# Layer norms as two fused VectorE operations, and the second expert result added by an accumulating DMA

## The chip, the cores and the metric

One core of one Trainium2 chip runs the whole program. The metric is device microseconds of one execution, as the median of several. The core has five engines that work side by side, each through its own instructions in order: TensorE (PE, whose weight loads are listed as PEld), VectorE (DVE), ScalarE (ACT), GpSimd (POOL) and SyncE (SP), which here only starts transfers. SP, ACT and POOL can all start DMAs; those of POOL have a queue of their own.

## What is computed

Two layers on 2048 tokens of 1024 numbers. Each layer has a mixer and then a mixture of experts, and after each of the two a residual and a layer norm. The first mixer is attention, the second a pooling over the last 2, 4, 8 or 16 tokens. Cut to what matters here:

```python
def layer_norm(x, g, b):
    mu = jnp.mean(x, axis=-1, keepdims=True)
    var = jnp.mean(jnp.square(x - mu), axis=-1, keepdims=True)
    return (x - mu) * lax.rsqrt(var + LN_EPS) * g + b

for i in range(2):
    f = mla_mixer(x, ...) if i == 0 else pool_mixer(x, ...)
    x = layer_norm(ALPHA * x + f, ln_g[i, 0], ln_b[i, 0])
    f = hier_moe(x, ...)          # two experts of 64 for each token, their results weighted and added
    x = layer_norm(ALPHA * x + f, ln_g[i, 1], ln_b[i, 1])
```

## The kernel before

The work runs in stages, one after the other: projections, attention, `output_projection`, the experts of layer 0, `pool_layer`, the experts of layer 1, `last_norm`. `output_projection` and `pool_layer` go over 16 tiles of 128 tokens. A tile's work is a Python generator; `run_slots` starts one tile every three slots and advances all of them one step per slot, so that the steps of some nine tiles are interleaved. A scheduler behind the program then puts each engine's instructions into one order, and buffers (`bufs=` of a tile) decide how far loads may run ahead.

The experts write their two weighted results for a token to two halves of a table `Y` in HBM. `pool_layer` does the following for a tile.

- `residual` (L1093) loads the two results (`rya`, `ryb`) and the residual (`rx`) with three DMAs on SP. POOL adds `ryb` to `rya` (L1103). DVE makes `rya = ALPHA*rx + rya` and the row sums (L1106).
- `normalize` (L968): DVE turns the sum into minus the mean (`lnnm`), ACT squares `rya - mean` and sums (L978), DVE makes the inverse deviation `lnrs` (L980 and `rsqrt`, L197: three Newton steps on 128x1 columns), then `lnnb = lnnm*lnrs` (L983), and ACT writes the normalized tile (L985).
- POOL multiplies the normalized tile by `ag` into `pres` (L1194). PE pools it with band matrices (`rpt`, L1201 and L1204), ACT copies that (`pooled`, L1206), PE multiplies it by the pool weights (`pz`, L1212 and L1216), and DVE adds it to `pres` in two halves (L1218).
- The second norm `n2` (class `Norm`, L988) is `normalize` on `pres` with a multiplication by `lng` on POOL (L1003; on DVE for the last tile alone) and an addition of `lnb` on DVE (L1005). The result is stored from ACT's queue.
- PE transposes the result (L1015), and the router (L496) chooses experts: a matmul (`plog`, L501), and some twenty small DVE instructions (`lg` to `ov`, L504 to L570) with two exponentials on ACT, a running count `ohsum` on POOL (L552) and a table on PE (`ptab`, L572).

`output_projection` uses the same `Norm` and the same router, and `last_norm` has the fused norm already, with `rsqrt`. While the last tiles of `pool_layer` run, SP loads the weights of three experts of layer 1.

Of the kernel before, what the change touches and what calls it, by code (L numbers as in the profile page):

```python
# [63 lines left out]
LN_EPS = 1e-5  # L64
# [132 lines left out]
def rsqrt(nc, pool, v):  # L197

    e, n = nc.vector, v.shape[1]
    y = pool.tile([P, n], I32, name="rsq_y", bufs=4)  # L200
    e.tensor_scalar(y, v.bitcast(I32), -0.5, 1597463007.0, op0=ALU.mult, op1=ALU.add)
    yf = y.bitcast(F32)
    h = pool.tile([P, n], F32, name="rsq_h", bufs=4)
    e.tensor_scalar(h, v, -0.5, None, op0=ALU.mult)
    t = pool.tile([P, n], F32, name="rsq_t", bufs=4)
    for i in range(3):
        if n == 1:
            e.tensor_scalar(t, yf, yf, h, op0=ALU.mult, op1=ALU.mult)
# [756 lines left out]
        self.ctx.close()  # L965


def normalize(nc, w, z, total):  # L968

    nm = w.tile([P, 1], F32, name="lnnm", bufs=4)  # L970
    if total.shape[1] == 2:
        nc.vector.tensor_scalar(nm, total[:, 0:1], total[:, 1:2], -1.0 / D, op0=ALU.add, op1=ALU.mult)
    else:
        nc.vector.tensor_scalar(nm, total, -1.0 / D, None, op0=ALU.mult)
    yield
    sq = w.tile([P, D], BF16, name="lnsq", bufs=1)
    rs = w.tile([P, 1], F32, name="lnrs", bufs=4)
    nc.scalar.activation(sq, z, AF.Square, bias=nm, accum_out=rs)  # L978
    yield
    nc.vector.tensor_scalar(rs, rs, 1.0 / D, LN_EPS, op0=ALU.mult, op1=ALU.add)  # L980
    rsqrt(nc, w, rs)
    nb = w.tile([P, 1], F32, name="lnnb", bufs=4)
    nc.vector.tensor_tensor(nb, nm, rs, op=ALU.mult)  # L983
    yield
    nc.scalar.activation(z, z, AF.Identity, bias=nb, scale=rs)  # L985


class Norm:  # L988
# [7 lines left out]
        queue.dma_start(self.g, g.partition_broadcast(P))  # L996
        queue.dma_start(self.b, b.partition_broadcast(P))

    def __call__(self, dst, z, total, engine=None):
        nc = self.nc  # L1000
        yield from normalize(nc, self.work, z, total)
        yield
        (engine or nc.gpsimd).tensor_tensor(z, z, self.g, op=ALU.mult)  # L1003
        yield
        nc.vector.tensor_tensor(dst, z, self.b, op=ALU.add)  # L1005


def transposed(nc, c, ps, work, x, out):
# [32 lines left out]
def output_projection(tc, c, I, wo, OT, X1, rt_pool, prefetch):  # L1041

    nc = tc.nc
    with ExitStack() as ctx:
# [13 lines left out]
        def token_tile(t):  # L1058
            sl = slice(t * P, (t + 1) * P)
            o = os[t % 2]  # L1060
            if t:
                wo.load(o, OT, t)
            z = w.tile([P, D], F32, name="z", bufs=4)
            loads.append(nc.sync.dma_start(z, I["x"][sl, :]))
            total = w.tile([P, 2], F32, name="total", bufs=4)
            yield
            for half in range(2):
                pz = ps.tile([P, 512], F32, name="pz", bufs=3)
                hs = slice(half * 512, half * 512 + 512)
                n = 0  # L1070
                for k in range(ND):
                    for a, b in ((0, 0), (1, 0), (0, 1)):
                        nc.tensor.matmul(pz, o[:, a, k, :], wo.parts[k][b][:, hs], start=(n == 0), stop=(n == 3 * ND - 1))  # L1073
                        n += 1
                yield
                nc.vector.scalar_tensor_tensor(z[:, hs], z[:, hs], ALPHA, pz, op0=ALU.mult, op1=ALU.add,
                                               accum_out=total[:, half:half + 1])
            yield from norm(z, z, total, nc.vector if t == NT - 1 else None)
            nc.scalar.dma_start(X1[sl, :], z)
            yield  # L1080
            xT = []
# [11 lines left out]
def residual(nc, w, X, Y, sl, out, loads):  # L1093
# [1 line left out]
    t0 = sl.start  # L1095
    ya = w.tile([P, D], F32, name="rya", bufs=6)
    nc.sync.dma_start(ya, Y[sl, :])
    yb = w.tile([P, D], F32, name="ryb")
    loads.append(nc.sync.dma_start(yb, Y[t0 + S:t0 + S + P, :]))
    x = w.tile([P, D], F32, name="rx")  # L1100
    nc.sync.dma_start(x, X[sl, :])
    yield
    nc.gpsimd.tensor_tensor(ya, ya, yb, op=ALU.add)  # L1103
    yield
    total = w.tile([P, 1], F32, name="rtotal", bufs=4)
    nc.vector.scalar_tensor_tensor(ya, x, ALPHA, ya, op0=ALU.mult, op1=ALU.add, accum_out=total)  # L1106
# [66 lines left out]
def pool_layer(tc, c, I, mixer, X1, Y, X3, rt_pool, prefetch):  # L1173

    nc = tc.nc
    with ExitStack() as ctx:
# [8 lines left out]
        def token_tile(t):  # L1185
# [5 lines left out]
            yield from normalize(nc, w, x2, total)  # L1191
            yield
            r = w.tile([P, D], F32, name="pres", bufs=4)
            nc.gpsimd.tensor_tensor(r, x2, ag, op=ALU.mult)  # L1194
            pp = w.tile([P, ND, P], F32, name="pooled")
            for half in range(2):
                pt = ps1.tile([P, 4, P], F32, name="rpt", bufs=2)
# [11 lines left out]
            for half in range(2):  # L1209
# [7 lines left out]
                yield  # L1217
                nc.vector.scalar_tensor_tensor(r[:, hs], pz.rearrange("p a b -> p (a b)"), 1.0, r[:, hs],  # L1218
                                               op0=ALU.mult, op1=ALU.add, accum_out=total[:, half:half + 1])
            yield from n2(r, r, total, nc.vector if t == NT - 1 else None)  # L1220
            nc.scalar.dma_start(X3[sl, :], r)
            yield
            xT = []
# [310 lines left out]
def last_norm(tc, c, Y, xs, norm, out):  # L1534

    nc = tc.nc
    with tc.tile_pool(name="fin", bufs=3, reuse_waits="tile") as w, tc.tile_pool(name="fin_ps", bufs=4, space=PSUM, reuse_waits="tile") as ps:

        def pair(n):
# [26 lines left out]
                nc.scalar.activation(sq, z[:, i], AF.Square, bias=nm[:, i:i + 1], accum_out=rs[:, i:i + 1])  # L1566
                nc.vector.scalar_tensor_tensor(o[:, i], z[:, i], nm[:, i:i + 1], norm.g, op0=ALU.add, op1=ALU.mult)
            yield
            nc.vector.tensor_scalar(rs, rs, 1.0 / D, LN_EPS, op0=ALU.mult, op1=ALU.add)
            rsqrt(nc, w, rs)  # L1570
            for i in range(2):
                nc.vector.scalar_tensor_tensor(o[:, i], o[:, i], rs[:, i:i + 1], norm.b, op0=ALU.mult, op1=ALU.add)
                nc.scalar.dma_start(out[t0 + i * P:t0 + (i + 1) * P, :], o[:, i])
# [114 lines left out]
```

## Time and profile before

| | us |
|---|---|
| median of 3 runs (3017.34 to 3025.28) | 3017.5 |
| the profiled execution: its own time | 3011.0 |
| the profiled execution: from the first to the last instruction (the span) | 3009.2 |
| busy in the span: PE / DVE / POOL / ACT | 2675.4 / 1482.6 / 1029.1 / 861.0 |
| `output_projection`, from about 1200 to | 1448 |
| experts of layer 0, to about | 2052 |
| `pool_layer`, to about | 2320 |
| experts of layer 1, to about | 2893 |

Times in the profile are counted from the first instruction of one profiled execution. "Busy" is time in which an engine had an instruction in work; an instruction that is held up after it started counts as busy. The granted clock is TensorE's clock as a share of 2.4 GHz. A row of the timeline has the start, the duration, the engine, the line of the kernel and what is written and read; in square brackets stands how long the engine was idle before it and what ended that.

### The profile page before, as it was taken

The page shows a single profiled execution, that of the slowest core. Times are in us where ns is not written, and L with a number is a line of the kernel's source. Part 1 is how long each engine was busy: PE and PEld are TensorE (multiplying, and loading weights), DVE is VectorE, ACT ScalarE, POOL GpSimd, SP SyncE. Part 2 cuts the span into 40 slices and gives each one's busy share as a digit, 9 for nine tenths or more (in the row PEclk, how much of TensorE's full clock was granted, in tenths as well). Part 3 has the DMA queues.
Part 4 walks back from the last instruction along what each step waited for, and adds up shares of the span by engine and source line. Part 5 has one row for each costly group of instructions (what it writes and reads, how often), then busy time and mean ns, then how long its engine had stood idle before and what let it go on. Part 6 is the DMA issues. An engine that isn't in the chain of part 4 may idle for free.

```text
span 3009.2 us, 50823 instructions
## 1 busy us (share of the span) xinstructions
PE 2675.4 (89%) x19378; PEld 1499.0 (50%) x19378; DVE 1482.6 (49%) x3717; ACT 861.0 (29%) x1465; POOL 1029.1 (34%) x877
## 2 busy tenths in 40 slices
PE   6987988889889899999799998996887999999976
PEld 6874545545555455888333333334776333333323
DVE  7645767667778675446321111315997121111118
ACT  4444434344444434223111111113452111111102
POOL 4244656566666546211111111114542111111100
PEclk9998999999999999999799999997897999999989
DMA  6544122121221212646699999985415999999967
GB/s 206 192 153 161 58 71 68 61 75 59 78 71 58 68 33 88 189 144 231 253 419 417 411 410 358 419 353 217 161 64 232 359 419 417 414 409 411 417 263 289
DMA packets 230242, 690.22 MB, mean 229 GB/s; under 512 B 42318, under 2 KB 102990, under 8 KB 180588
## 3 DMA queue, kind: packets, MB, share of 16 engines
q1 hardware_dynamic: 191484, 586.01, 51.2%
q0 software_dynamic: 27104, 69.90, 6.1%
q10 hardware_dynamic: 11408, 31.02, 2.7%
q8 instruction: 155, 2.54, 0.3%
q14 instruction: 91, 0.75, 0.1%
HBM read 595.47 MB, written 120.71 MB: 238 GB/s over the span
## 4 chain that ended last, share of the span: by engine, by line
PE 55%; DMA 23%; DVE 13%; issue 4%; ACT 3%; POOL 2%; SPq 1%; ACTq 0%; DVEq 0%; POOLq 0%; another core or an unknown queue 0%
DMA w<-in_w_dram 15%; PE ph L1336 13%; PE sc L678 9%; PE py L1364 6%; PE po L678 6%; PE pz L1073 5%; PE pm L678 5%; DVE mx L800 3%; PE pt L1324 2%; PE pt L368 2%; PE pl L325 2%; PE plog L501 2%; DMA R<-rl 1%; DMA qn<-QN 1%; DMA rl<-R 1%
## 5 line engine op out<-in xcount | busy, mean ns | idle before, releaser
L1336 PE MATMUL ph<-w,xT 128*32 128x512 f32 x5888 | 680.5, 602 | 41.1 <-DMA w<-in_w_dram 41.0
L1336 PEld LDWEIGHTS ph<-w,xT 128*32 128x32 f32 x5888 | 198.9, 111 | 450.0 <-issue 427.3
L1293 POOL DMA_INDIRECT Y<-y,idst x92 | 91.9, 998 | 936.6 <-ACT xT L1325 874.5
L800 DVE TENSOR_REDUCE mx<-pm 128x2 f32<-128x1024 f32 (+2 forms) x320 | 339.5, 1061 | 116.1 <-PE pm L678 110.9
L903 POOL TENSOR_TENSOR acc<-acc,pe 128x512 f32<-128x512 f32 (+3 forms) x256 | 311.0, 1215 | 207.5 <-ACT pe L889 194.4
L889 ACT ACTIVATE pe<-sc 128x1024 f32<-128x1024 f32 (+1 forms) x320 | 280.0, 896 | 355.7 <-DVE sc L887 202.2
L1341 DVE SCALAR_TENSOR_TENSOR h<-sg,gate,ph 128x256 f32<-128x256 f32 x92 | 44.2, 480 | 658.8 <-ACT sg L1339 658.8
L1364 PE MATMUL py<-w,hT 128*32 128x512 f32 x2944 | 347.9, 592 | 1.6 <-DVE hT L1351 1.6
L678 PE MATMUL sc<-qn,k 64*128 64x512 f32 (+2 forms) x1920 | 260.1, 376 | 20.8 <-ACT rl L846 15.5
L678 PE MATMUL po<-pe,vt 128*64 128x512 f32 (+3 forms) x1280 | 277.8, 557 | 0.0
L1339 ACT ACTIVATE sg<-ph 128x256 f32<-128x256 f32 x92 | 35.4, 384 | 727.0 <-PE ph L1336 715.0
L902 DVE TENSOR_TENSOR acc<-acc,pe 128x512 f32<-128x512 f32 (+3 forms) x256 | 226.3, 884 | 11.0 <-ACT pe L889 10.0
L1364 PEld LDWEIGHTS py<-w,hT 128*32 128x32 f32 x2944 | 106.1, 110 | 214.3 <-issue 210.1
L678 PEld LDWEIGHTS sc<-qn,k 64*128 64x128 f32 x1920 | 176.8, 195 | 66.7 <-ACT rl L846 20.6
L678 PE MATMUL pm<-k,qn 64*128 64x512 f32 (+2 forms) x640 | 146.4, 451 | 70.0 <-DVE mx L800 64.4
L1366 DVE COPY y<-py 128x512 f32<-128x512 f32 x92 | 63.6, 692 | 224.4 <-PE py L1364 224.4
L678 PEld LDWEIGHTS pm<-k,qn 64*128 64x128 f32 x640 | 64.7, 194 | 188.6 <-DVE mx L800 98.8
L678 PEld LDWEIGHTS po<-pe,vt 128*64 128x64 f32 x1280 | 80.3, 140 | 131.8 <-issue 123.5
L1324 PEld LDWEIGHTS pt<-ident,xg 128*128 128x128 f32 x736 | 90.4, 194 | 97.4 <-issue 72.9
L1324 PE MATMUL pt<-ident,xg 128*128 128x128 f32 x736 | 108.2, 291 | 23.2 <-DMA xg<-X,isrc 21.9
L678 PE MATMUL pm<-ka,qa 64*128 64x512 f32 (+2 forms) x640 | 124.9, 382 | 0.0
L678 PE MATMUL sc<-qb,kb 33*128 33x512 f32 (+2 forms) x640 | 121.4, 371 | 0.0
(364 smaller groups left out, 4331.3 us busy)
## 6 DMA issues: line engine op xcount, KB each, us to landing
w<-in_w_dram SPq DMA_DIRECT2D x384, 1024.0 KB
fy<-Y SPq DMA_DIRECT2D x16, 1024.0 KB
OT<-ot SPq DMA_DIRECT2D x31, 512.0 KB
K<-kq SPq DMA_DIRECT2D x32, 256.0 KB
V<-v SPq DMA_DIRECT2D x16, 512.0 KB
QN<-kq SPq DMA_DIRECT2D x32, 256.0 KB
qn<-QN SPq DMA_DIRECT2D x32, 256.0 KB
qb<-QR SPq DMA_DIRECT2D x128, 64.0 KB
```

The costliest lines, as they stand in the source:

```text
L325: nc.tensor.matmul(pl, a[:, k, :], w[:, k, :], start=(k == 0 and n == 0), stop=(k == ND - 1 and n == 2))
L678: return self.pin(self.nc.tensor.matmul(*a, **kw))
L800: self.pin(nc.vector.tensor_reduce(mx[:, :, tt, ch], pm[:, :, :n], axis=AX.X, op=ALU.max))
L889: nc.scalar.activation(pe[:, :, c0:], sc[:, :, c0:], AF.Exp, scale=SCALE)
L902: self.pin(self.nc.vector.tensor_tensor(acc[:, 0, c0:], before[:, 0, c0:], pe[:, 0, c0:], op=ALU.add))
L903: self.nc.gpsimd.tensor_tensor(acc[:, 1, c0:], before[:, 1, c0:], pe[:, 1, c0:], op=ALU.add)
L1073: nc.tensor.matmul(pz, o[:, a, k, :], wo.parts[k][b][:, hs], start=(n == 0), stop=(n == 3 * ND - 1))
L1293: st = self.nc.gpsimd.indirect_dma_start(out=self.Y, out_offset=bass.IndirectOffsetOnAxis(ap=idx, axis=0), in_=y, in_offset=None, bounds_c ...
L1324: self.pin(nc.tensor.transpose(pt[:, j, :], x[:, half * 4 + j, :], self.c.ident))
L1336: self.pin(nc.tensor.matmul(ph[js], xT[:, k, js], w[:, :, k, :], start=(k == 0), stop=(k == ND - 1), tile_position=(0, j * n)))
L1364: self.pin(nc.tensor.matmul(py[js], hT[:, k, js], w[:, k, hs], start=(k == 0), stop=(k == NF - 1), tile_position=(0, j * n)))
L1366: (nc.vector.tensor_copy if half else nc.scalar.copy)(y[:, hs], py)
```

## The change

The norms of class `Norm` (the one in `output_projection` and the second one in `pool_layer`) lose the ACT pass that normalizes: `(z - mean)*g` and `(..)*rs + b` are each one DVE instruction. Everywhere the inverse deviation starts from a scaled column and needs one DVE instruction less. In `pool_layer` the multiplication by `ag` goes from POOL to DVE, and the addition of the second expert result is no instruction of an engine any more: a DMA started by POOL adds it to `rya` in place, once the first result has landed there.

```diff
+def inverse_deviation(nc, pool, v):
+    e, n = nc.vector, v.shape[1]
+    h = pool.tile([P, n], F32, name="rsq_h", bufs=4)
+    e.tensor_scalar(h, v, -0.5 / D, -0.5 * LN_EPS, op0=ALU.mult, op1=ALU.add)
+    y = pool.tile([P, n], I32, name="rsq_y", bufs=4)
+    e.tensor_scalar(y, h.bitcast(I32), -0.5, 519526879.0, op0=ALU.mult, op1=ALU.add)
...
-def normalize(nc, w, z, total):
+def minus_mean(nc, w, total):
     nm = w.tile([P, 1], F32, name="lnnm", bufs=4)
...
+def squares(nc, w, z, nm):
...
     nc.scalar.activation(sq, z, AF.Square, bias=nm, accum_out=rs)
+    return rs
+
+def normalize(nc, w, z, total):
+    nm = minus_mean(nc, w, total)
     yield
-    nc.vector.tensor_scalar(rs, rs, 1.0 / D, LN_EPS, op0=ALU.mult, op1=ALU.add)
-    rsqrt(nc, w, rs)
+    rs = squares(nc, w, z, nm)
+    yield
+    inverse_deviation(nc, w, rs)
...
-    def __call__(self, dst, z, total, engine=None):
+    def __call__(self, dst, z, total):
         nc = self.nc
-        yield from normalize(nc, self.work, z, total)
+        nm = minus_mean(nc, self.work, total)
         yield
-        (engine or nc.gpsimd).tensor_tensor(z, z, self.g, op=ALU.mult)
+        rs = squares(nc, self.work, z, nm)
         yield
-        nc.vector.tensor_tensor(dst, z, self.b, op=ALU.add)
+        inverse_deviation(nc, self.work, rs)
+        nc.vector.scalar_tensor_tensor(z, z, nm, self.g, op0=ALU.add, op1=ALU.mult)
+        nc.vector.scalar_tensor_tensor(dst, z, rs, self.b, op0=ALU.mult, op1=ALU.add)
...
     nc.sync.dma_start(ya, Y[sl, :])
-    yb = w.tile([P, D], F32, name="ryb")
-    loads.append(nc.sync.dma_start(yb, Y[t0 + S:t0 + S + P, :]))
+    nc.gpsimd.dma_start(ya, Y[t0 + S:t0 + S + P, :], accum_op=ALU.add)
     x = w.tile([P, D], F32, name="rx")
-    nc.sync.dma_start(x, X[sl, :])
+    loads.append(nc.sync.dma_start(x, X[sl, :]))
     yield
-    nc.gpsimd.tensor_tensor(ya, ya, yb, op=ALU.add)
     yield
...
             r = w.tile([P, D], F32, name="pres", bufs=4)
-            nc.gpsimd.tensor_tensor(r, x2, ag, op=ALU.mult)
+            nc.vector.tensor_tensor(r, x2, ag, op=ALU.mult)
...
             yield
-            nc.vector.tensor_scalar(rs, rs, 1.0 / D, LN_EPS, op0=ALU.mult, op1=ALU.add)
-            rsqrt(nc, w, rs)
+            inverse_deviation(nc, w, rs)
```

The scheduler orders the changed program anew. On POOL, in the middle of `pool_layer`, this was one tile's work before, from one running count `ohsum` to the next:

```order
L552 TENSOR_TENSOR ohsum_19083<-ohsum_19083,ohb 128x64
L1003 TENSOR_TENSOR pres<-pres,lng_19073 128x1024
L1103 TENSOR_TENSOR rya<-rya,ryb 128x1024
L1194 TENSOR_TENSOR pres<-rya,ag 128x1024
L552 TENSOR_TENSOR ohsum_19083<-ohsum_19083,ohb 128x64
```

And this is POOL in the changed program, from the start of the stage on (the lines are those of the changed file; L1128 is the accumulating DMA, L571 the running count):

```order
628 L1128 DMA rya<-Y_62 128x1024 x9
629 L571 TENSOR_TENSOR ohsum_19016<-ohsum_19016,ohb 128x64
630 L1128 DMA rya<-Y_62 128x1024 x2
631 L571 TENSOR_TENSOR ohsum_19016<-ohsum_19016,ohb 128x64
632 L1128 DMA rya<-Y_62 128x1024
```

The three wide instructions per tile are gone, and the running counts stand behind DMA starts, the first one behind nine of them.

On DVE, in the middle of the stage, this is a piece of one tile's work before: router instructions (`es` to `oh`, and `ohp`, `ov`), with the addition of `lnb` and the two additions to `pres` and `rya` between them.

```order
2466 L523 TENSOR_REDUCE es<-esel 128x8
2467 L568 TENSOR_SCALAR ohp<-iota,rpos_19086 128x192
2468 L525 MAX em<-es 128x8
2469 L570 TENSOR_TENSOR ov<-oh,rval_19087 128x128
2470 L527 MAX_INDEX ei<-em,es 128x8
2471 L1005 TENSOR_TENSOR pres<-pres,lnb_19074 128x1024
2472 L529 SCALAR_TENSOR_TENSOR rexp_19085<-gf,ei 128x2
2473 L1218 SCALAR_TENSOR_TENSOR pres,ptotal<-pz,pres 128x512
2474 L533 TENSOR_SCALAR nem<-em 128x1
2475 L546 TENSOR_SCALAR oh<-iota,rexp_19085 128x64 x2
2476 L980 TENSOR_SCALAR lnrs<-lnrs 128x1
2477 L1106 SCALAR_TENSOR_TENSOR rya,rtotal<-rx,rya 128x1024
```

And a piece of one tile's work in the changed program, with the multiplication by `ag` (L1222) and the first of the two fused operations of the norm (L1034; the second, L1035, stands 20 rows on):

```order
2413 L1222 TENSOR_TENSOR pres<-rya,ag 128x1024
2414 L525 MAX gm<-lg 128x8
2415 L583 SCALAR_TENSOR_TENSOR rk,rpos_19019<-oh,plog 128x64
2416 L527 MAX_INDEX gi<-gm,lg 128x8
2417 L533 TENSOR_SCALAR ngm<-gm 128x1
2418 L583 SCALAR_TENSOR_TENSOR rk,rpos_19019<-oh,plog 128x64
2419 L529 CAST gf<-gi 128x1
2420 L219 TENSOR_SCALAR rsq_h<-lnrs 128x1
2421 L1034 SCALAR_TENSOR_TENSOR pres<-pres,lnnm,lng_19006 128x1024
2422 L531 TENSOR_SCALAR goh<-iota,gf 128x8
2423 L222 TENSOR_SCALAR rsq_y<-rsq_h 128x1
2424 L1246 SCALAR_TENSOR_TENSOR pres,ptotal<-pz,pres 128x512
```

Two 1024-wide instructions per tile stood here; now there are four (L1134, which is L1106 of before, L1222, L1034 and L1035), and the instructions of `lnrs` stand between them and the router's.

## Rows read from the trace of the kernel before

**Rows 1.** Windows view: busy us (instructions) of PE, PEld, DVE, ACT, POOL; clock, DMA share, GB/s.

```profile
1276.00:1348.00 72.00, 72.00 (x398) 62.27 (x397) 36.02 (x227) 21.52 (x46) 13.78 (x11) 1.00 0.49 149
2052.00:2144.60 92.60, 68.20 (x393) 60.11 (x393) 73.47 (x213) 40.45 (x63) 54.77 (x23) 0.80 0.64 233
2144.60:2221.20 76.60, 61.10 (x383) 53.93 (x381) 76.56 (x292) 37.02 (x73) 37.70 (x20) 0.91 0.35 122
2221.20:2320.00 98.80, 82.30 (x500) 74.31 (x498) 87.11 (x434) 42.87 (x90) 29.61 (x23) 0.84 0.42 167
2320.00:2893.00 573.00, 544.00 (x4807) 201.67 (x4807) 104.42 (x225) 71.34 (x136) 89.81 (x90) 0.98 0.95 388
```

**Rows 2.** The timeline of DVE in the middle of `pool_layer`.

```profile
2144.63 1.21 DVE L1106 SCALAR_TENSOR_TENSOR rya<-rx,rya 128x1024 f32<-128x1024 f32 x1
...
2152.55 2.38 DVE L520 TENSOR_TENSOR esel<-lg,goh 128x64 f32<-128x64 f32 x1
...
2221.16 1.22 DVE L1106 SCALAR_TENSOR_TENSOR rya<-rx,rya 128x1024 f32<-128x1024 f32 x1
```

**Rows 3.** The timeline of POOL at the same place.

```profile
2152.37 2.48 POOL L1103 TENSOR_TENSOR rya<-rya,ryb 128x1024 f32<-128x1024 f32 x1
```

**Rows 4.** Groups of DVE in the same 76.6 us: xcount | busy us, mean ns | idle before.

```profile
L568 DVE TENSOR_SCALAR ohp<-iota,rpos 128x192 f32<-128x192 f32 x10 | 15.3, 1528 | 0.0
L520 DVE TENSOR_TENSOR esel<-lg,goh 128x64 f32<-128x64 f32 x5 | 9.6, 1929 | 0.0
...
L512 DVE TENSOR_SCALAR goh<-iota,gf 128x8 f32<-128x8 f32 x5 | 7.4, 1488 | 0.0
...
L570 DVE TENSOR_TENSOR ov<-oh,rval 128x128 f32<-128x128 bf16 x10 | 7.0, 697 | 0.0
```

**Rows 5.** The same groups of DVE in five tiles of `output_projection`.

```profile
L568 DVE TENSOR_SCALAR ohp<-iota,rpos 128x192 f32<-128x192 f32 x10 | 3.1, 307 | 0.0
L570 DVE TENSOR_TENSOR ov<-oh,rval 128x128 f32<-128x128 bf16 x10 | 2.8, 285 | 0.0
...
L212 DVE SCALAR_TENSOR_TENSOR rsq_y<-rsq_t,rsq_y 128x1 f32<-128x1 f32 x10 | 1.5, 147 | 0.0
L520 DVE TENSOR_TENSOR esel<-lg,goh 128x64 f32<-128x64 f32 x5 | 1.4, 271 | 0.0
...
L512 DVE TENSOR_SCALAR goh<-iota,gf 128x8 f32<-128x8 f32 x5 | 1.1, 228 | 0.0
```

**Rows 6.** Groups of DVE in the whole of `pool_layer`.

```profile
L568 DVE TENSOR_SCALAR ohp<-iota,rpos 128x192 f32<-128x192 f32 x30 | 25.0, 835 | 0.0
...
L212 DVE SCALAR_TENSOR_TENSOR rsq_y<-rsq_t,rsq_y 128x1 f32<-128x1 f32 x64 | 21.8, 342 | 0.4
...
L570 DVE TENSOR_TENSOR ov<-oh,rval 128x128 f32<-128x128 bf16 x30 | 16.6, 562 | 0.5 <-PE plog L550 0.3
L512 DVE TENSOR_SCALAR goh<-iota,gf 128x8 f32<-128x8 f32 x16 | 15.9, 995 | 0.0
L520 DVE TENSOR_TENSOR esel<-lg,goh 128x64 f32<-128x64 f32 x16 | 12.5, 782 | 0.0
```

**Rows 7.** Groups of DVE in `last_norm`.

```profile
L1567 DVE SCALAR_TENSOR_TENSOR fo<-fy,fnm,w 128x1024 f32<-128x1024 f32 x16 | 20.3, 1281 | 0.0
```

**Rows 8.** The timeline of SP and DVE at the start of `pool_layer`.

```profile
2051.89 0.34 SPq L1097 DMA_DIRECT2D rya<-Y  x1
...
2062.22 1.23 DVE L1106 SCALAR_TENSOR_TENSOR rya<-rx,rya 128x1024 f32<-128x1024 f32 x1 [14.66 <-POOL rya L1103]
```

**Rows 9.** The tile view of `xg` (indirect gathers of 512 KB, started by POOL).

```profile
L1287 POOL DMA_INDIRECT xg<-X,isrc x92: 988/1020/1162, 1448.3 to 2849.2; - x92
...
DMA to landing us min/median/max: 7.2/9.1/13.4
```

**Rows 10.** The chain of waits, pieces at the start of `pool_layer`: start us, us, what.

```profile
2063.93 2.34 POOL rya L1103
...
2091.67 2.38 POOL pres L1003
```

More of the change, by code (lines that the diff above doesn't have):

```diff
@@ L204, in rsqrt @@
     e.tensor_scalar(h, v, -0.5, None, op0=ALU.mult)
+    t = pool.tile([P, n], F32, name="rsq_t", bufs=4)
+    for i in range(3):
+        if n == 1:
+            e.tensor_scalar(t, yf, yf, h, op0=ALU.mult, op1=ALU.mult)
+        else:
+            e.tensor_tensor(t, yf, yf, op=ALU.mult)
+            e.tensor_tensor(t, t, h, op=ALU.mult)
+        e.scalar_tensor_tensor(v if i == 2 else yf, t, 1.5, yf, op0=ALU.add, op1=ALU.mult)
+def inverse_deviation(nc, pool, v):
[4 more added lines that the diff above has]
+    e.tensor_scalar(y, h.bitcast(I32), -0.5, 519526879.0, op0=ALU.mult, op1=ALU.add)
+    yf = y.bitcast(F32)
     t = pool.tile([P, n], F32, name="rsq_t", bufs=4)
@@ L974, in normalize @@
         nc.vector.tensor_scalar(nm, total, -1.0 / D, None, op0=ALU.mult)
-    yield
+    return nm
+def squares(nc, w, z, nm):
     sq = w.tile([P, D], BF16, name="lnsq", bufs=1)
@@ L1077, in token_tile @@
                                                accum_out=total[:, half:half + 1])
-            yield from norm(z, z, total, nc.vector if t == NT - 1 else None)
+            yield from norm(z, z, total)
             nc.scalar.dma_start(X1[sl, :], z)
@@ L1219, in token_tile @@
                                                op0=ALU.mult, op1=ALU.add, accum_out=total[:, half:half + 1])
-            yield from n2(r, r, total, nc.vector if t == NT - 1 else None)
+            yield from n2(r, r, total)
             nc.scalar.dma_start(X3[sl, :], r)
```

## The prediction, made before the changed kernel was run

> **What bounds the kernel now.** I read the windows view first, stage by stage, to see where the change can matter. In five tiles of `output_projection` TensorE is busy 72.00 of 72.00 us at the full clock, and DVE half of that: PE is the bound. In the middle of `pool_layer`, from 2144.6 to 2221.2, it is the other way round: DVE is busy 76.56 of 76.6 us, PE 61.10 at a granted clock of 0.91 (toward 2.4 GHz, as in the other stages of this view). The experts of layer 1 (573 us) are busy on PE for 544.00 and move 388 GB/s with a DMA share of 0.95 [rows 1]. So only `pool_layer`, 2052 to 2320, can answer much to this change, and since the experts start when it ends and are full throughout, its gain should reach the end undiminished.
>
> Then I asked what DVE's busy time in that stretch consists of. The timeline has the sums L1106 of tiles five apart at 2144.63 and 2221.16: 76.5/5 = 15.3 us per tile. A 64-wide addition, L520, takes 2.38 us at 2152.55 [rows 2], and in the same 2.4 us POOL runs a 1024-wide addition, L1103, of 2.48 us, begun at 2152.37 [rows 3]. The two end together. A group table shows that this is the rule: in these five tiles L568 takes 1528 ns in the mean, L520 1929, L512 1488, L570 697 [rows 4]. In `output_projection`, where POOL is busy 13.78 of 72 us only, the same instructions take 307, 271, 228 and 285 [rows 5]. DVE is not working there; it is held by POOL's wide instructions, three in each tile. The reader should see that "busy" in rows 4 is mostly waiting.
>
> **The change, part by part.**
>
> *POOL's three wide instructions go.* The excess of the four groups over their undisturbed durations is, for five tiles, 10×(1.528−0.307) + 5×(1.929−0.271) + 5×(1.488−0.228) + 10×(0.697−0.285) = 12.2 + 8.3 + 6.3 + 4.1 = 30.9 us [rows 4, 5], that is 6.2 us per tile. For the whole stage, with L212 added: 30×0.528 + 30×0.277 + 16×0.767 + 16×0.511 + 64×0.195 = 15.8 + 8.3 + 12.3 + 8.2 + 12.5 = 57.1 us [rows 5, 6], so 26.2 us lie outside the middle stretch. On POOL stay the 16 running counts (short) and 16 starts of DMAs; no row shows these starts holding DVE.
>
> *DVE gets wide work.* Per tile: one multiplication by `ag`, priced as the 1024-wide L1106, 1.22 us [rows 2]; two fused operations at 1.28 us, the price of `last_norm`'s fused line L1567 [rows 7]; away go the addition of `lnb` (again 1.22) and three instructions on one column at 0.147, the undisturbed L212 [rows 5], one of them in each `lnrs` and one in `lnnb`. Together 1.22 + 2.56 − 1.22 − 0.44 = +2.1 us per tile.
>
> *The middle stretch.* DVE would need 15.3 − 6.2 + 2.1 = 11.2 us per tile. PE needs 61.1/5 = 12.2 at clock 0.91, and 12.2×0.91 = 11.1 at full clock [rows 1]. The two are nearly level, so neither will be filled perfectly. With PE fuller, I expect a higher clock, as in `output_projection`; so I take a period of 11.8 us, between the two. Five tiles then take 59 us in place of 76.6: **−17.5**. Ends: −20 (11.2 us held perfectly, with a little rounding off PE), and −7 if PE stays at 0.80, the clock of the 92.6 us before [rows 1]: 11.1/0.80 = 13.9 us per tile.
>
> *Fill and drain*, the other 11 tiles: the stalls of 26.2 us go; at the start the chain of waits runs through POOL itself, eight pieces from 2063.93 (2.34 us) to 2091.67 (2.38 us), 18.9 us in all [rows 10], which go too; DVE's new work costs 11×2.1 = 23.5. Sum **−21.6**. Lower end −3 (26.2 − 23.5, if others take the chain's pieces over: ACT's passes and DVE's new ones stand in the same places). Upper end −46: POOL is busy 54.77 + 29.61 = 84.4 us in these two windows [rows 1], of which 0.82 (2.0 of 2.45 us per instruction, as in rows 2 and 3) could be stall, 69 − 23.5.
>
> *The accumulating DMA.* Before, `ryb` is loaded beside `rya`; now it starts when `rya` has landed, so two transfers stand in a row. The nearest rows of a POOL-started 512 KB transfer are the gathers `xg`: POOL is held 988/1020/1162 ns for a start, and 7.2/9.1/13.4 us pass to landing [rows 9]. In the middle of the stage the loads run about two tiles (24 us) ahead through six buffers `rya`, which covers two transfers. At the start nothing covers them: the first load starts at 2051.89, and the first L1106 at 2062.22 after one L1103 [rows 8], so both loads had landed by 2059.9. Load and accumulate in a row would give at most 2059.9 + 9.1 = 2069, against 2062.2: +7; at best the plain load is short enough that nothing is lost: 0. I take **+4**. POOL's queue: the first running count stands behind nine accumulate starts, so the first router may wait a few us for a later tile's load; it has many slots until its result is used, and I cost it at nothing. SP keeps two loads per tile instead of three.
>
> A rule bears on these starts. The Trainium skill, "DMA: Bandwidth & Descriptors", section "🔬 Anatomy of one DMA — SWDGE (gpsimd) path", gives 2.0 us plus the bytes at 436 GB/s for such a transfer, an estimate of 3.2 us for 512 KB; the gathers here take nearly three times that, and by it the start would lose about 1 us, and the sum would be 3 us lower.
>
> *Elsewhere.* `output_projection` stays PE-bound, and only its last tile's norm becomes shorter by one ACT pass: −1 (ends −2 and +1). `last_norm` loses eight one-column instructions of 0.15 us, beside wide work: 0. ACT loses 16 passes in each of two stages, and ACT is busy at most 42.87 of 98.8 us in the stage [rows 1]: 0.
>
> **Sum.** −17.5 − 21.6 + 4 − 1 = −36. The profiled execution took 3011.0 us, so 2975; the median of the runs is 6.5 us above it, so about **2981 us**. A measurement of this kernel can tell some 0.3%, 9 us, from no change.
>
> **Rivals.**
>
> *The gain in full (0.15).* DVE and PE interleave with no gap, period 11.2, and the fill gains up to its upper end: −20 − 38 + 2 − 1 = −57, about 2960, and 2952 at the extreme. For it: a busy share of 1.00 on DVE in the middle before. Against: DVE and PE level is a poor case for that.
>
> *PE becomes the bound at a low clock (0.13).* The clock is 0.80 and 0.84 in the outer windows [rows 1]; if the router's waits keep PE in short bursts, the tile costs 13.9 us: −7 −11 + 3 = −15, about 3002.
>
> *The accumulating DMA paces the stage (0.11, slower).* No row shows one. If each must read both operands through the same 16 engines and the next waits for the last, 2×9.1 = 18.2 us per tile, 16×18.2 + 10 to fill = 301 us against 268: +33, about 3050. It decides from 268/16 = 16.75 us per tile on. For it: all sixteen stand in one queue, and each holds one of six buffers until it lands. Against: gathers `xg` are moved beside 388 GB/s of weights [rows 1, 9], and here the DMA share is 0.35.
>
> A page names another way to the same end. The Trainium skill, "SBUF — State Buffer", section "🔬 SBUF: two separate sides", says that a DMA issued from GpSimd cannot get its descriptors written while DVE is in a mode that locks the shared port. In a stage where DVE is always full this would delay every start. In rows: starts take 1020 ns with DVE busy 18% (104.42 of 573) [rows 1, 9], and no row has them beside a full DVE. The longest DVE instruction is 1.3 us, so 16 starts lose some 20 us on POOL, which has little else to do; this gives 0 alone and only the rival's time if starts queue up.
>
> *No change (0.06).* The stalls are not POOL's doing, or the DMA starts hold DVE as the additions did; then −30.9 becomes +2.1 per tile less the chain's gain, near 3015.
>
> The forecast itself has 0.55. Of the low-clock rival a small part ends within 0.3%. Faster: 0.55 + 0.15 + 0.12 = 0.82; within 0.3%: 0.07; slower: 0.11. The range takes in the forecast, the full gain and the low clock: 2952 to 3006.
>
> **What would show it.** Right: no wide instruction on POOL; L568 (now L587), L520 (L539), L512 (L531) and L570 (L589) near 0.31, 0.27, 0.23 and 0.29 us in the middle; L1134 (L1106 before) every 11 to 12 us; L1222 near 1.22, L1034 and L1035 near 1.28 each; PE above 0.9 busy there, clock over 0.91; first L1134 some 4 us later into the stage; experts of layer 1 as long as before (573 us). Wrong: L1134 waiting for the DMA into `rya` in mid-stage, with landings of more than 12 us; DVE's short instructions long beside POOL's DMA starts; the clock at 0.80; or a stage that ends 35 us earlier and experts that are longer by as much.

## The result, and the profile after

| | before | changed |
|---|---|---|
| median of 4 runs each (range), us | 3019.8 (3017.3 to 3025.3) | 2966.2 (2963.3 to 2968.7) |
| the profiled execution, us | 3011.0 | 2968.7 |
| ratio of the runs, 95% interval | | 0.982 [0.980, 0.984] |

The change makes the kernel 53.6 us faster; the forecast of 2981 stood for 36. The two profiled executions lie 42.3 us apart, and these the traces explain; the profiled execution before is 6.3 us shorter than the shortest of its four runs, and the 11.3 us by which the medians lie further apart are in no trace.

Where the time went is counted from the first load of `rya` to the first gather of layer 1, two rows in the timelines of SP and POOL of the changed kernel:

```profile
2054.79 0.34 SPq L1127 DMA_DIRECT2D rya<-Y  x1
...
2282.45 1.10 POOL L1315 DMA_INDIRECT xg<-X,isrc  x1 [5.67 <-issue]
```

This is "the stage" below: 227.7 us here; before it ran from 2051.89 [rows 8] to 2325.80, 273.9 us. So 46.2 us come from `pool_layer` (the windows below are cut to tenths, so that the changed kernel's stage is 227.6 there). What follows the stage is as long as before (684.1 against 683.4 us), so the gain reaches the end undiminished.

The windows view of the changed kernel (columns as in [rows 1]: length, then PE, PEld, DVE, ACT, POOL, clock, DMA share, GB/s): the whole stage, then its four parts.

```profile
2054.80:2282.40 227.60, 189.80 (x1322) 172.60 (x1322) 189.67 (x939) 102.99 (x209) 28.09 (x35) 0.88 0.70 220
```

```profile
2054.80:2103.40 48.60, 25.56 (x141) 22.70 (x142) 25.45 (x84) 15.87 (x24) 6.17 (x7) 0.68 0.94 279
2103.40:2142.40 39.00, 38.99 (x290) 36.63 (x289) 34.90 (x169) 23.26 (x45) 4.91 (x6) 1.00 0.70 182
2142.40:2206.20 63.80, 63.80 (x469) 60.24 (x468) 62.98 (x325) 36.79 (x76) 10.82 (x11) 1.00 0.63 173
2206.20:2282.40 76.20, 61.45 (x428) 53.04 (x427) 66.34 (x366) 27.07 (x66) 6.20 (x11) 0.85 0.60 243
```

From 2103 to 2206 PE is busy 102.79 of 102.8 us at the full clock, where before DVE was the full engine at a PE clock of 0.91 [rows 1]. DVE is still at 62.98 of 63.8. Both are full, as the forecast's two figures, 11.1 and 11.2 us, implied. In the whole stage PE's 1322 matmuls take 189.8 us; before they took 214.1. Half of the gain (24.3 us) is PE doing the same work at a higher clock, the other half (22.0) is PE idle less, 37.8 us in place of 59.8. The clock has two levels in both traces, 0.50 and 1.00. Before, it stood at the lower one in nine stretches of the stage; first comes the sum of these nine in the windows view, then the only two of the changed kernel, at the start and at the end:

```profile
sum 89.70, PE 63.44 PEld 56.55 DVE 67.41 ACT 27.67 POOL 32.84; mean PE 7.05 PEld 6.28 DVE 7.49 ACT 3.07 POOL 3.65
```

```profile
2054.80:2086.00 31.20, 8.16 (x26) 6.54 (x27) 11.19 (x40) 7.14 (x11) 5.31 (x6) 0.50 0.99 299
2260.00:2282.40 22.40, 12.70 (x93) 10.31 (x93) 15.47 (x91) 2.74 (x10) 3.63 (x6) 0.50 0.70 283
```

PE was busy at the half clock for 63.4 us before and for 20.9 us after. Half of the difference, some 21 us of the 24.3, is what the clock gave back (an estimate from these rows).

Where in the stage the gain lies can be read from the last instruction of the second norm, that of the first and that of the last tile, before and then in the changed kernel:

```profile
2094.07 3.35 DVE L1005 TENSOR_TENSOR pres<-pres,lnb 128x1024 f32<-128x1024 f32 x1 [2.33 <-POOL pres L1003]
...
2301.04 1.22 DVE L1005 TENSOR_TENSOR pres<-pres,lnb 128x1024 f32<-128x1024 f32 x1
```

```profile
2099.20 1.27 DVE L1035 SCALAR_TENSOR_TENSOR pres<-pres,lnrs,lnb 128x1024 f32<-128x1024 f32 x1
...
2259.39 1.28 DVE L1035 SCALAR_TENSOR_TENSOR pres<-pres,lnrs,lnb 128x1024 f32<-128x1024 f32 x1
```

The norm of the first tile is done 45.5 us after the first load before and 45.7 us after it in the changed kernel. The last one is done 204.8 and 160.2 us later, and then 23.5 and 21.8 us pass to the first gather. So 44.6 of the 46.2 us are the interval between tiles, 13.7 us before and 10.7 in the mean of all sixteen, and the two ends of the stage gained next to nothing. That speaks against a rival which the experiments below call the shorter path: that it pays at the two ends that a tile has fewer steps which wait for another engine.

The groups of DVE in the stage answer to [rows 4, 6, 7]:

```profile
L1035 DVE SCALAR_TENSOR_TENSOR pres<-pres,lnrs,lnb 128x1024 f32<-128x1024 f32 x16 | 20.4, 1277 | 0.0
L1034 DVE SCALAR_TENSOR_TENSOR pres<-pres,lnnm,lng 128x1024 f32<-128x1024 f32 x16 | 20.4, 1276 | 0.0
...
L1222 DVE TENSOR_TENSOR pres<-rya,ag 128x1024 f32<-128x1024 f32 x16 | 19.5, 1219 | 0.0
L587 DVE TENSOR_SCALAR ohp<-iota,rpos 128x192 f32<-128x192 f32 x32 | 10.0, 312 | 0.1
...
L589 DVE TENSOR_TENSOR ov<-oh,rval 128x128 f32<-128x128 bf16 x32 | 9.1, 285 | 0.3 <-PE plog L569 0.3
...
L539 DVE TENSOR_TENSOR esel<-lg,goh 128x64 f32<-128x64 f32 x16 | 4.2, 260 | 0.0
...
L531 DVE TENSOR_SCALAR goh<-iota,gf 128x8 f32<-128x8 f32 x16 | 3.6, 224 | 0.0
```

The four short instructions are back at the durations of [rows 5] (307, 285, 271, 228), and the added wide ones cost what they were priced at. The sums L1134 of two tiles in the middle show the new period, 11.04 us per tile against 15.3:

```profile
2165.39 1.22 DVE L1134 SCALAR_TENSOR_TENSOR rya<-rx,rya 128x1024 f32<-128x1024 f32 x1
...
2176.43 1.22 DVE L1134 SCALAR_TENSOR_TENSOR rya<-rx,rya 128x1024 f32<-128x1024 f32 x1
```

At the start of the stage, the first accumulating DMA starts on POOL 4.0 us after the first load, and the first sum on DVE 13.7 us after it; before that was 10.3 [rows 8]:

```profile
2058.77 1.00 POOL L1128 DMA_DIRECT2D rya<-Y  x1 [6.58 <-DMA rya<-Y]
...
2068.44 1.22 DVE L1134 SCALAR_TENSOR_TENSOR rya<-rx,rya 128x1024 f32<-128x1024 f32 x1 [17.98 <-DMA rx<-X]
```

The row puts the wait down to the load of `rx`. The first accumulate, the slowest of the view below with 9.7 us, landed at the same moment (2058.77 + 9.7 = 2068.5).

And the tile view of `rya` has all sixteen of them, with their landing:

```profile
L1128 POOL DMA_DIRECT2D rya<-Y x16: 856/866/1002, 2058.8 to 2188.0; - x16
...
DMA to landing us min/median/max: 5.3/7.0/9.7
```

### The profile page after: what moved, and what is told of

Same layout as the page of the kernel before. It is cut to its first block, busy times and chain, and to the rows that moved or that the text cites. A ratio compares the mean times of both kernels' runs of the same rounds, so it can differ in the third digit from the quotient of the medians.

```text
span 2966.5 us, 50666 instructions
## 1 busy us (share of the span) xinstructions
PE 2657.1 (90%) x19378; PEld 1482.6 (50%) x19378; DVE 1454.7 (49%) x3675; ACT 823.2 (28%) x1433; POOL 897.4 (30%) x831
## 3 DMA queue, kind: packets, MB, share of 16 engines
q1 hardware_dynamic: 189180, 577.62, 51.3%
## 4 chain that ended last, share of the span: by engine, by line
PE 57%; DMA 23%; DVE 12%; issue 3%; ACT 2%; POOL 1%; SPq 0%; ACTq 0%; DVEq 0%; POOLq 0%; another core or an unknown queue 0%
DMA w<-in_w_dram 15%; PE ph L1364 14%; PE sc L697 9%; PE po L697 6%; PE py L1392 6%; PE pz L1103 6%; PE pm L697 5%; DVE mx L819 3%; PE pt L1352 2%; PE pt L387 2%; PE pl L344 2%; PE plog L520 1%; PE pz L1244 1%; DMA R<-rl 1%; DMA qn<-QN 1%
## 5 line engine op out<-in xcount | busy, mean ns | idle before, releaser
L921 DVE TENSOR_TENSOR acc<-acc,pe 128x512 f32<-128x512 f32 (+3 forms) x256 | 236.9, 925 | 11.0 <-ACT pe L908 10.0
L1392 PEld LDWEIGHTS py<-w,hT 128*32 128x32 f32 x2944 | 106.5, 110 | 214.2 <-issue 214.1
L697 PEld LDWEIGHTS sc<-qn,k 64*128 64x128 f32 x1920 | 176.9, 194 | 65.3 <-ACT rl L865 20.9
```

The source lines that it names most:

```text
L697: return self.pin(self.nc.tensor.matmul(*a, **kw))
L921: self.pin(self.nc.vector.tensor_tensor(acc[:, 0, c0:], before[:, 0, c0:], pe[:, 0, c0:], op=ALU.add))
L1392: self.pin(nc.tensor.matmul(py[js], hT[:, k, js], w[:, k, hs], start=(k == 0), stop=(k == NF - 1), tile_position=(0, j * n)))
```

## The experiments

"Stage" is as above; PE busy and clock are those of the windows view over the stage, and idle is the difference. "First" is the time from the first load to the end of the first tile's second norm, and "interval" the mean distance from one tile's second norm to the next one's. The ratios are to the kernel before.

| kernel | stage | first | interval | PE busy | PE idle | clock | median | ratio, 95% interval |
|---|---|---|---|---|---|---|---|---|
| before | 273.9 | 45.5 | 13.66 | 214.1 | 59.8 | 0.84 | 3019.8 | |
| changed | 227.6 | 45.7 | 10.68 | 189.8 | 37.8 | 0.88 | 2966.2 | 0.982 [0.980, 0.984] |
| undo_acc | 244.7 | 40.1 | 12.19 | 203.5 | 41.2 | 0.85 | 2988.2 | 0.990 [0.987, 0.992] |
| undo_ag | 249.3 | 46.9 | 12.04 | 199.8 | 49.5 | 0.86 | 2994.1 | 0.990 [0.988, 0.993] |
| undo_norm | 256.9 | 52.1 | 12.13 | 202.3 | 54.6 | 0.85 | 2991.5 | 0.990 [0.987, 0.992] |
| spare_pool | 239.2 | 56.6 | 10.72 | 191.8 | 47.4 | 0.87 | 2981.6 | 0.986 [0.984, 0.989] |
| spare_pool_late | 264.7 | 47.3 | 13.05 | 210.9 | 53.8 | 0.82 | 2999.4 | 0.992 [0.990, 0.995] |
| add_on_dve | 229.6 | 39.0 | 11.26 | 191.2 | 38.4 | 0.90 | 2971.2 | 0.983 [0.980, 0.985] |
| no_ag | 235.7 | 46.0 | 11.23 | 197.0 | 38.7 | 0.86 | 2971.0 | 0.983 [0.979, 0.986] |
| start_plain | 228.2 | 45.5 | 10.68 | 190.9 | 37.3 | 0.89 | 2967.7 | 0.982 [0.979, 0.984] |
| plain6 | 222.2 | 39.7 | 10.74 | 190.0 | 32.2 | 0.89 | 2958.4 | 0.979 [0.976, 0.982] |
| plain9 | 223.2 | 39.1 | 10.75 | 189.1 | 34.1 | 0.90 | 2961.9 | 0.980 [0.976, 0.984] |
| norm_only | 255.2 | 43.2 | 12.69 | 204.1 | 51.1 | 0.85 | 2992.5 | 0.991 [0.988, 0.994] |
| short_rsqrt_only | 278.4 | 44.9 | 13.99 | 215.7 | 62.7 | 0.83 | 3020.4 | 1.000 [0.999, 1.001] |

### Does a wide POOL instruction cost DVE time that nobody waits for?

Two kernels add POOL work to the changed kernel and nothing else. The first:

```diff
             nc.vector.tensor_tensor(r, x2, ag, op=ALU.mult)
+            spare = w.tile([P, D], F32, name="spare", bufs=1)
+            nc.gpsimd.tensor_tensor(spare, ag, ag, op=ALU.mult)
```

> The changed kernel, with one more 1024-wide multiplication on POOL per tile of pool_layer that writes a scratch tile; nothing reads it and its operands are ready from the start. Stall: it holds a short DVE instruction for about 2.07 us each time, 16 x 2.07 = 33 us: a stage of about 260, some 3000 us, with the rows of short DVE instructions showing means well over their 0.2 to 0.3 us. Shorter path: nobody waits for it, a stage of 228 to 230; at most POOL's DMA starts stand 2.4 us behind it.

The stage rose by 11.6 us, between the two theories, and the timeline of POOL says why the run tells little:

```profile
2059.16 7.81 POOL L1224 TENSOR_TENSOR spare<-ag 128x1024 f32<-128x1024 f32 x4 [3.34 <-issue]
...
2094.03 11.84 POOL L1224 TENSOR_TENSOR spare<-ag 128x1024 f32<-128x1024 f32 x5
```

With operands ready from the start, all sixteen ran in the first 48 us of the stage, some ahead of the accumulating DMAs in POOL's queue. In the middle the period stayed at 11.0; the first tile was done 10.9 us later, and that is nearly all of the loss. So the second reads the normalized tile, `nc.gpsimd.tensor_tensor(spare, x2, ag, op=ALU.mult)` with two buffers, which puts it where the tile is worked on.

> The changed kernel, with one more 1024-wide multiplication per tile on POOL, of the normalized tile into a scratch tile that nothing reads; since it reads the normalized tile, it runs where the tile is worked on, in the full middle of the stage, not ahead of it. Stall: the period of the middle rises from 11.0 to about 13.1 us per tile, one DVE instruction per tile takes over 2 us, and the stage is 244 to 257 us, some 2985 to 2995 us. Shorter path: nobody waits for its result, period 11.0 as before, stage 228 to 231.

The stage rose by 37 us, more than either theory gave. Two of the sixteen, from the timelines of POOL and of DVE:

```profile
2157.76 2.34 POOL L1224 TENSOR_TENSOR spare<-rya,ag 128x1024 f32<-128x1024 f32 x1 [1.90 <-ACT rya L1013]
...
2170.90 2.35 POOL L1224 TENSOR_TENSOR spare<-rya,ag 128x1024 f32<-128x1024 f32 x1
```

```profile
2157.78 2.33 DVE L557 TENSOR_TENSOR den<-ps,gs 128x1 f32<-128x1 f32 x1
...
2170.93 2.33 DVE L557 TENSOR_TENSOR den<-ps,gs 128x1 f32<-128x1 f32 x1
```

L557 is a multiplication of 128x1 numbers that takes 0.15 us in the changed kernel. Here it begins 0.02 to 0.03 us after POOL's instruction and ends with it. The distances between the sums are 13.1 to 16.7 us in the middle. Nothing reads `spare`, and DVE has the same 939 instructions, whose busy time rose by 29.8 us to 219.5, 1.9 us for each of the sixteen. So the shorter path can't explain this: the stall is shown. The price was more than these 29.8 us: PE, now idle between DVE's results, ran at a lower clock, and its own busy time rose from 189.8 to 210.9 us.

```profile
2056.90:2321.60 264.70, 210.92 (x1322) 190.69 (x1322) 219.51 (x939) 103.16 (x209) 65.70 (x51) 0.82 0.58 179
```

The Trainium skill, "SBUF — State Buffer", section "Who interferes with whom", says that a DVE instruction with two inputs in SBUF contends with a GpSimd instruction that reads SBUF. The rows agree: L557 has two. That sentence does not cover L565 of undo_acc below, nor L568 and L512 of [rows 4], which have one tensor input and a column; that these are held too is shown by their rows alone.

### Each part undone

`undo_acc`:

```diff
-    nc.gpsimd.dma_start(ya, Y[t0 + S:t0 + S + P, :], accum_op=ALU.add)
+    yb = w.tile([P, D], F32, name="ryb")
+    loads.append(nc.sync.dma_start(yb, Y[t0 + S:t0 + S + P, :]))
...
+    nc.gpsimd.tensor_tensor(ya, ya, yb, op=ALU.add)
```

> The changed kernel, with the second expert result loaded plainly again and added by POOL. The stage is counted from the first load of rya to the first gather of layer 1: 273.9 us before, 227.7 in the changed kernel. Theory of the stall (a wide POOL instruction holds one short DVE instruction for 2.07 us, and DVE is full): DVE needs 11.0 + 2.07 us per tile, 16 x 2.07 = 33 us more, less up to 4 us at the start: a stage of about 257, some 2995 us. Rival, the shorter path (what pays is that a tile has fewer steps that wait for another engine, at the two ends of the stage): up to three additions of 2.4 us on the chain and the start's gain against them, a stage of 225 to 233.

`undo_ag`:

```diff
-            nc.vector.tensor_tensor(r, x2, ag, op=ALU.mult)
+            nc.gpsimd.tensor_tensor(r, x2, ag, op=ALU.mult)
```

> The changed kernel, with the multiplication by ag on POOL again. Stall: DVE gets 2.07 us of being held and loses 1.22 us of work per tile, 16 x 0.85 = 14 us: a stage of about 241, some 2980 us. Shorter path: one piece of 2.4 in place of 1.2 us a few times, a stage of 228 to 232.

`undo_norm`: class `Norm` as in the kernel before.

> The changed kernel, with the norms of before (ACT pass, multiplication by lng on POOL, addition of lnb on DVE), but the shorter inverse deviation. Stall: per tile 2.07 held + 1.22 for lnb + 0.15 for lnnb - 2 x 1.28 = +0.9 us on DVE, 16 x 0.9 = 14 us: a stage of about 242, some 2981 us. Shorter path: an ACT pass and a POOL instruction more on each tile's chain, 1.24 + 2.4 us at the two ends only: a stage of 229 to 236. Output_projection about 2 us longer in both.

In undo_acc the period is 13.0 us in the mean (five gaps of the middle, 12.5 to 13.4), where 11.0 + 2.07 was expected, and the timelines show the pair:

```profile
2178.36 2.35 POOL L1133 TENSOR_TENSOR rya<-rya,ryb 128x1024 f32<-128x1024 f32 x1 [8.64 <-DMA rya<-Y]
```

```profile
2178.62 2.15 DVE L565 TENSOR_SCALAR oh<-iota,rexp 128x64 bf16<-128x64 f32 x1
```

The stage rose by 17 us, not 29: the first tile was done 5.6 us earlier, and in the mean of all tiles the interval grew by 1.5 us, not by the 2.07 of the middle. Undo_ag cost 21.7 us and undo_norm 29.3, where the stall alone gave some 14 for each, and the shorter path at most 9: both theories missed these two. DVE's busy time rose by 10.3 and 10.9 us, no more than the stall gave; PE's rose by 10.0 and 12.5 us, at a lower clock, and its idle time by 11.7 and 16.8. The tiles of both lie 12.0 to 12.1 us apart in the mean, where 10.7 + 0.9 = 11.6 was to be expected (the sums of undo_norm lie 11.8 and 12.0 apart in two places of the middle, but 29.7 and 23.0 just before). Of undo_norm's 29.3 us, 6.4 lie before the first tile is done. How its idle time divides between the ACT pass and the wait for POOL in each norm wasn't separated; its `output_projection` was no longer than in the changed kernel, against the expectation.

The three losses add up to 68 us for a change that gained 46.2. So the parts don't add: what one is worth depends on which of the others are there. Why the sum comes out above the whole, and not below it, no run shows.

### Parts alone

Norms alone, on the kernel before, and of these the shorter inverse deviation alone:

```diff
-    nc.vector.tensor_scalar(rs, rs, 1.0 / D, LN_EPS, op0=ALU.mult, op1=ALU.add)
-    rsqrt(nc, w, rs)
+    inverse_deviation(nc, w, rs)
```

> The kernel before, with the fused norms and the shorter inverse deviation alone; the additions of the second result and the multiplication by ag stay on POOL, so two wide POOL instructions per tile are left. Stall alone: 0.9 us per tile from the norm and 0.3 from the two shorter inverse deviations, period 14.1, stage 273.9 - 16 x 1.2 = about 255, some 3000 us. If the shorter path at the end counts beside it, as undo_norm suggests (its drain from the last sum to the first gather was 75.8 us, 62.4 in the changed kernel): another 10 to 13 us, stage 242 to 246.

> The kernel before with the shorter inverse deviation alone: one DVE instruction of 0.15 us less in each of two norms per tile, in a stage in which DVE is full: 16 x 0.3 = 5 us, a stage of about 269 and 3015 us; POOL's three wide instructions are all there, so at most one stall per tile fewer can be hit. If nothing but the removal of POOL's work counts: 273 to 275.

Norm_only gave 255.2 us, as the stall alone would have it, 18.7 less than before. The shorter inverse deviation gave nothing: its ratio is 1.000, and its stage 278.4 where 269 was expected. DVE's busy time in it was 242.8 us, not less than before's 240.4. That fits a queue in which the held instructions set the pace; no run shows it by itself.

### Which engine sets the new period?

```diff
-            nc.vector.tensor_tensor(r, x2, ag, op=ALU.mult)
+            nc.scalar.copy(r, x2)
```

> The changed kernel, with ACT copying the normalized tile into pres in place of DVE's multiplication by ag: the factor ag is left out. It takes 1.22 us per tile from DVE and gives ACT some 1.24. If DVE sets the period: 9.8 us per tile, the stage up to 16 x 1.2 = 19 us shorter, 208 to 215. If TensorE does: period 11.0 as before, stage 225 to 228.

And the second result added on DVE (`nc.vector.tensor_tensor(ya, ya, yb, op=ALU.add)` behind a plain load):

> The changed kernel, with the second expert result loaded plainly and added by DVE (1.22 us) in place of the accumulating DMA. If DVE sets the period of 11.0: 12.2 us per tile, the stage 3 us earlier at its start and 16 x 1.22 = 20 us longer behind it: about 244, some 2983 us. If TensorE sets the period and DVE has slack that its busy time hides: period 11.0 to 11.3, stage 225 to 230, no slower than the changed kernel; the accumulating DMA then bought nothing over this.

The same 62 us of the middle in the windows view, add_on_dve first:

```profile
2144.00:2206.00 62.00, 58.63 (x414) 52.85 (x413) 62.00 (x288) 31.99 (x69) 6.90 (x6) 1.00 0.49 166
```

```profile
2144.00:2206.00 62.00, 62.00 (x453) 58.46 (x453) 54.09 (x297) 40.47 (x78) 7.61 (x11) 1.00 0.68 179
```

With 1.22 us more on DVE the period is 12.2, DVE full; with 1.22 less PE is full at 62.00 and does 453 matmuls in that time, the rate of the changed kernel (469 in 63.80 us, in the windows above); its tiles lie 11.2 us apart in the mean, not 9.8. So in the middle of the changed kernel TensorE is the bound, at its full clock, and DVE has next to nothing to spare. Neither expectation was met as written: add_on_dve has the longer period of the one branch and the stage of the other, since the middle is a part of the stage only. No_ag's stage came out 8 us longer than the changed kernel's, and 7.2 of it is PE's busy time, at a clock of 0.86; in the changed kernel PE filled up once and stayed full.

### What the accumulating DMA costs

Add_on_dve has a period 1.2 us longer and yet a stage only 2.0 us longer, because its start is faster: the first sum stands 9.4 us after the first load, not 13.7. In the runs the two can hardly be told apart (medians of 2971.2 and 2966.2, intervals that overlap): over an addition on DVE the accumulating DMA bought next to nothing. The page's table of DMA queues says more (packets, MB, share of 16 engines' span), the changed kernel first:

```profile
q1 hardware_dynamic: 189180, 577.62, 51.3%
q0 software_dynamic: 29408, 78.29, 7.8%
```

```profile
q1 hardware_dynamic: 191484, 586.01, 52.2%
q0 software_dynamic: 27104, 69.90, 6.1%
```

The same 8.39 MB are 7.8% of 2966.5 less 6.1% of 2972.2 = 50 us of all engines as accumulates, and 52.2% less 51.3% of the same = 30 us as plain loads. The shares are rounded to 0.1%, which is some 3 us, and the time of q1 differs by up to 11 us between kernels with the same bytes. So the means over all kernels are the better figures: between the five that load everything plainly and the six that accumulate everything, q0 differs by 49 us and q1 by 22. Accumulates take about twice what plain loads take. In the first 49 us of the stage the changed kernel's DMA share is 0.94 at 279 GB/s, and add_on_dve moves as much at 0.77:

```profile
2058.80:2107.80 49.00, 31.64 (x196) 28.45 (x197) 36.47 (x117) 19.93 (x31) 0.00 (x0) 0.77 0.77 279
```

So the accumulates are the dear ones, and with them the fill of the stage looks bound by transfers. That suggests plain loads at the start, where DVE has room:

```diff
-    nc.gpsimd.dma_start(ya, Y[t0 + S:t0 + S + P, :], accum_op=ALU.add)
+    early = t0 < 3 * P
+    if early:
+        yb = w.tile([P, D], F32, name="ryb", bufs=2)
+        nc.sync.dma_start(yb, Y[t0 + S:t0 + S + P, :])
+    else:
+        nc.gpsimd.dma_start(ya, Y[t0 + S:t0 + S + P, :], accum_op=ALU.add)
...
     yield
+    if early:
+        nc.vector.tensor_tensor(ya, ya, yb, op=ALU.add)
     yield
```

> The changed kernel, with the first three tiles of the stage loading the second expert result plainly and adding it on DVE, which is idle then; the other thirteen accumulate by DMA. If the accumulate behind the load is what delays the start: the first sum L1134 about 10.3 to 11.5 us after the first load instead of 13.7, and, with TensorE full from then on, the stage 2 to 4 us shorter: 224 to 226. If the fill is bound by the transfers themselves (DMA share 0.94 there): no gain, 227 to 229.

The first sum came at 9.5 us, and the stage did not get shorter: 228.2; its first tile is done at 45.5 us, as late as in the changed kernel. The windows from 20 to 50 us into the stage show where it was lost; first the changed kernel, then start_plain:

```profile
2074.80:2084.80 10.00, 5.74 (x21) 5.09 (x22) 6.83 (x26) 5.11 (x8) 1.71 (x2) 0.50 1.05 286
2084.80:2094.80 10.00, 10.00 (x67) 9.26 (x66) 7.86 (x21) 4.36 (x6) 0.00 (x0) 0.94 0.77 218
2094.80:2104.80 10.00, 10.00 (x65) 9.15 (x65) 8.86 (x35) 6.56 (x11) 0.86 (x1) 1.00 0.83 249
```

```profile
2076.30:2086.30 10.00, 10.00 (x62) 9.45 (x62) 7.53 (x26) 4.55 (x8) 0.88 (x1) 0.87 1.02 253
2086.30:2096.30 10.00, 9.01 (x57) 7.86 (x56) 4.55 (x11) 4.74 (x8) 1.69 (x2) 1.00 0.93 208
2096.30:2106.30 10.00, 6.69 (x31) 5.39 (x31) 9.18 (x36) 5.52 (x8) 0.84 (x1) 0.83 0.79 214
```

PE is full ten us earlier, and starves twenty us later: the first accumulated tiles are late (DVE waits 2.31 and 5.41 us for `rya` there). So more tiles plain, six and nine:

> As start_plain, with the first six tiles loaded plainly and added on DVE. There the gain at the start (first sum 9.5 us after the first load, not 13.7) was lost again where the first accumulated tile came: PE busy only 15.7 of 20 us, 30 to 50 us into the stage, with a DMA share of 0.8 to 0.9. If late transfers are the cause: with six plain tiles the loads have got ahead by then, PE stays full from 20 us into the stage, 221 to 225 us. If DVE's six additions (7 us) are what costs: 227 to 230.

> As plain6, with nine tiles plain. Late transfers: as plain6 or better by 1 us, less 3 x 1.22 us of DVE in a part where DVE is at 9 of 10: 221 to 227. DVE's additions: 229 to 232, near add_on_dve's 229.6.

```profile
2073.80:2083.80 10.00, 10.00 (x61) 9.33 (x59) 8.69 (x27) 4.03 (x6) 0.00 (x0) 0.81 0.75 280
2083.80:2093.80 10.00, 9.83 (x61) 8.49 (x60) 10.00 (x32) 7.39 (x11) 1.00 (x1) 1.00 0.84 201
2093.80:2103.80 10.00, 10.00 (x75) 9.31 (x74) 9.05 (x39) 5.19 (x10) 0.88 (x1) 1.00 0.66 156
```

This is plain6 in the same place: PE stays full. Its stage is 222.2 us, 5.4 less than the changed kernel's, all of it idle time of PE; its first tile is done 6.0 us earlier, and the interval is nearly the same. Plain9 has 223.2. Late transfers, the first theory of both expectations, are borne out. The four runs of plain6 (2950.4 to 2961.9) lie under those of the changed kernel (2963.3 to 2968.7), but the two come from different sets of runs and the intervals of their ratios overlap: that plain6 is the faster one rests on the stage in the traces.

## Why the prediction was right, step by step

- **Bound and stall: right.** The mechanism that carried the forecast, POOL's wide instructions holding DVE, is shown by spare_pool_late; the four groups fell to the durations taken from `output_projection`. The prices of DVE's new work (1.22, 1.28, 1.28) were met to 0.01 us.
- **Middle stretch: mis-sized.** Taken was a period of 11.8 us (−17.5); measured 11.0, 5 × (15.3 − 11.0) = −21.5. The step that failed is "so neither will be filled perfectly": PE and DVE at 11.1 and 11.2 do interleave with no gap, and the clock goes to 1.00, not to something between 0.91 and 1.00. The rival of the full gain described the middle, and its 2960 us lies nearer to the measured 2966 than the forecast's 2981.
- **Fill and drain: mis-sized.** Of the stage's 46.2 us, 21.5 are the middle's and 3.3 were lost at the start, so the rest gained 28.0, where −21.6 was taken. That this is near is in part luck, since two terms were off in opposite directions. The eight pieces of the chain at the start were to give 18.9 us: from the first sum to the end of the first tile's second norm 35.2 us passed before and 32.0 in the changed kernel, a gain of 3.2. And the stalls were more than the 57.1 us counted from five groups: DVE's busy time in the stage was 240.4 us before and 189.7 after, with some 16 × 2.1 = 34 us more work, so it was held for some 85 us in all (an estimate from these numbers). The gain is in the interval between tiles, and not at the ends. Outside the middle the forecast did not count either that PE's own work would shrink by the clock, in the whole stage from 214.1 to 189.8 us.
- **The accumulating DMA: right in size, incomplete in kind.** +4 was taken for the first sum; it came 3.3 us later relative to the stage's start. Landing took 7.0 us (5.3 to 9.7), below the 9.1 of the gathers, and far from the 16.75 us per tile at which the slower rival would have decided. The Trainium skill, "DMA: Bandwidth & Descriptors", section "🔬 Anatomy of one DMA — SWDGE (gpsimd) path", gave the prediction an estimate of 3.2 us for such a transfer, by which the start would have lost about 1 us: here the measurement decides, against it. The loads ran further ahead than the 24 us that were taken: the tile summed at 2165.39 was loaded from 2128.4 on. That an accumulate takes more of the DMA engines than a plain load was not foreseen; plain6, which avoids it in six tiles, gains 5.4 us.
- **POOL's starts beside a full DVE:** five of the sixteen, from 2143.2 to 2188.0, stand in the stretch in which DVE is busy 62.98 of 63.8 us. They take 0.87 us each, like the others (856/866/1002 ns) and no longer than the 988/1020/1162 of the gathers [rows 9]. So the second mechanism of the slower rival, starts held by DVE, does not show.
- **Elsewhere:** −1 was taken for `output_projection`; no run here resolves it. What follows the stage is unchanged (+0.7), as forecast.
- **The total.** The profiled execution was put at 2975 and took 2968.7. The rest of the 15 us between 2981 and 2966 is the step from the profiled execution to the median: 6.5 us were added, as before; in the changed kernel the profiled execution is 2.5 above the median. Code ahead of `output_projection` that is the same in all kernels took from 1192.5 to 1202.4 us until its first matmul, so differences of this size between executions are not the change's.
- **Sums and readings.** 11 × 2.1 is 23.1, not 23.5, which changes nothing. The −11 of the low-clock rival is not derived. The 3015 of the rival "no change" does not follow from its terms: 16 × 2.1 = 34 us of new work, less 18.9 for the chain, is slower by some 15 us. L520, called an addition, is a multiplication.

## What to carry to other kernels

A short instruction whose mean is several times its own duration elsewhere can be waiting and not work, and the engine that is "full" by its busy time may be held by a neighbour: compare the same form in a stage where the neighbour is quiet, before costing anything. Moving work from POOL to a full DVE can pay, because what it frees (6.2 us per tile for three wide instructions, 2.07 each; 1.9 in spare_pool_late) is more than what it adds (1.22). When an edit takes a wait from an engine that feeds TensorE, price TensorE's busy time at the full clock as well: here that was half of the gain, and in the undone versions two fifths to four fifths of the loss.

## What was not expected of the hardware

- An accumulating DMA of 512 KB takes some 49/16 = 3.1 us of all 16 engines, a plain load of the same size some 22/16 = 1.4, by the shares of the queues in eleven kernels (an estimate).
- PE's 1322 matmuls of one stage took from 189.1 to 215.7 us of busy time over these kernels, the shortest at a granted clock of 0.90, the longest at 0.83.
- A wide POOL instruction can hold a wide DVE instruction too: in spare_pool_late L1222, usually 1.22 us, took 3.24 to 3.59 us in three places beside POOL's 2.35 to 2.69, and it ends about 1.1 us after POOL's each time.
